# One value burst per head in sparse attention, memory-attention outputs in the transposing banks, keys and queries evicted raw

## The chip, the cores and the metric

The kernel runs on one core of one Trainium2 chip. A core has five engines that run side by side, each in its own program order: TensorE (PE; its weight loads are shown as PEld), VectorE (DVE), ScalarE (ACT), GpSimd (POOL) and SyncE (SP), which issues most of the weight DMAs. TensorE writes its results to PSUM, which has eight banks of 128 x 512 float32; ACT and DVE take them from there to SBUF. The metric is the device time of one execution in microseconds. Three runs of the kernel before took 2106.66, 2106.75 and 2107.36 us; the median is 2106.75 us.

## The reference, cut to what matters

Two decoder layers over 512 tokens of width 1024. Each layer has a mixer of three branches (sparse attention "NSA", HGRN2, gated delta net), a cross attention over 256 memory tokens, and a gated MLP with a short convolution. The change touches the sparse attention and the memory attention:

```python
# sparse attention: 8 heads in 2 groups, head width 64
q = apply_rope(rmsnorm(q, q_norm));  k_* = apply_rope(rmsnorm(k_*, k_norm))   # k_cmp, k_sel, k_win
p_cmp = masked_softmax(q @ kc.T * scale);   o_cmp = p_cmp @ vc     # 31 compressed blocks
p_sel = masked_softmax(q @ k_sel.T * scale); o_sel = p_sel @ v_sel # top 16 of 8 blocks: all, causal
p_win = masked_softmax(q @ k_win.T * scale); o_win = p_win @ v_win # window 512: causal
o = g0 * o_cmp + g1 * o_sel + g2 * o_win
# memory attention: 4 heads of width 128, 256 memory tokens
q = rmsnorm(h @ w_q, q_norm); k = rmsnorm(mem_k, k_norm)
o = softmax(q @ k.T * scale) @ mem_v;  x = x + o @ w_o
# rmsnorm(x, g) = x * rsqrt(mean(x * x) + 1e-6) * g, and h itself is rmsnorm(x)
```

## The kernel before, in words

Activations are held feature-major: 128 features by 512 tokens a tile. A dense product (`dense`, `fm_proj`) splits each weight tile into a high and a low float32r part (`load_w`: the tile `wh` by ACT, `wl` by DVE) and each activation likewise (tiles `act`), and issues three 128x512 matmuls per 128 input features into a PSUM tile `pd`. The layer's first norm is not applied to the activations before the product: its factor per token is multiplied in when the product is evicted (`fm_scaled`: one DVE multiply of `pd` by the tile `rb`). `norm.r` holds the same factors as one column per block of 128 tokens.

PSUM is cut into three pools: `pd` has 3 banks (dense products), `pa` has 2 (attention scores, attention outputs, recurrences), `pt` has 3 (transposes and small sums).

The mixer runs the delta net, then HGRN2 woven with the key side of NSA (`nsa_pre`: head norms, rotary embedding, the compressing MLP, and the split of the keys into high and low parts `KH`, `KL`), then the projections of the gates and of the NSA queries (`nsa_queries`), one branch, then the attention (`nsa_attn`). The head norm (`head_rs`) squares the projected tiles on ACT, sums them with tiny matmuls, transposes the sums and takes a reciprocal square root with small DVE instructions.

`nsa_attn` goes over four blocks i of 128 queries and, in each, over four pairs j of heads (one head of each group g). Each step of j (called a head below; there are 32 in the two layers) has two branches `br` (selected, window) and two groups, so four score tiles: two matmuls and a mask matmul into `pa`, a maximum on DVE, an exponential on ACT into a tile `pr`, a scaling on DVE. Each `pr` is then transposed in 128x128 pieces into one `pt` bank, copied by ACT to a new tile `pT`, and used in the value products. The output bank `po` comes from `pa`; its first two products are those of the compressed branch (tile `vcpad`), then come those of the values (tile `tok`). Each value product fills 64 of the array's columns (`128*64` in the profile), and group 0 and group 1 use the two halves.

The order of instructions on each engine isn't written out by hand. A scheduling layer sets it from the dependencies, the ring of buffers of each pool and priorities: code under `tc.high_priority(...)` is put ahead of other ready work. Dense matmuls of the gate projections (`gate`) that don't depend on the attention are put between its steps.

`xattn` does the same with 4 heads over 256 memory tokens: `queries`, `attend`, `finish`. In `finish`, two `pt` banks take the transposed probabilities, DVE copies the first and ACT the second to SBUF, and the product with `memV` goes to a `pa` bank, from which `split` makes the high and low parts for the output projection.

The lines that the prediction follows: L235 is every matmul (`mm`), L242 every ACT activation (`act`), L245 every two-tensor operation, L254 every scalar-tensor-tensor, L1099 the transposes of the sparse attention, L1352 and L1353 transposes and copies of the memory attention.

Of the kernel before, what the change touches and what calls it, by code (L numbers as in the profile page):

```python
# [9 lines left out]
F32 = mybir.dt.float32  # L10
# [9 lines left out]
P = 128  # L20
T = 512
NT = T // P
# [176 lines left out]
def tile_trunk(ctx, tc, a, out, dbg=None):  # L199
# [47 lines left out]
    def ts(o, x, s1, s2, op0, op1=None, eng=None):  # L247
        if op1 is None:
            (eng or V).tensor_scalar(o, x, s1, None, op0)
        else:  # L250
            (eng or V).tensor_scalar(o, x, s1, s2, op0, op1)
# [159 lines left out]
            TE.transpose(ps[:, i * rw:(i + 1) * rw], rows[:, i * P:(i + 1) * P], ident[:rw, :rw])  # L411
        return ps[:, :n * rw].rearrange("p (i c k) -> p i c k", c=nt, k=32)[:, :, :, :nh]

    def head_rs(srcs, nh, scale, eps, post=1.0, nt=NT):
        n = len(srcs) * nt * nh
        v = small(n)
        ts(v.rearrange("p (i c h) -> p i c h", c=nt, h=nh), head_sums(srcs, nh, nt), scale, eps, MUL, ADD)
        return rsqrt(v, n, post=post)

    def spread(r, i, nh, nt=NT, ps=None):  # L420
        ps = pt() if ps is None else ps
# [23 lines left out]
    def fm_scaled(norm, src, o=None):  # L445
        ps = fm_proj(norm, src)
        o = chain() if o is None else o
        with tc.high_priority(PRI2):
            tt(o, ps, norm.rb, MUL)
        return o  # L450

    gdn_S = [cst.tile([P, P], F32, name=f"gdnS{i}") for i in range(2)]
# [452 lines left out]

    NSA_K, NSA_Q = ("nkc", "nvc", "nks", "nkw"), ("nq0", "nq1", "nq2", "nq3")

    def nsa_pre(l, st):
        mark("nsa")
        rope = [chain(), chain()]  # L910
        for i in range(2):
# [4 lines left out]
        raw = box["nsa"]  # L916

        def rope_norm(idx, gains, post):
            r = head_rs([raw[i] for i in idx], 2, 1.0 / 64, EPS, post)
            for n_, i in enumerate(idx):  # L920
                t_ = raw[i]
                stt(t_, t_, gains[n_], spread(r, n_, 2), MUL, MUL)
                sh = tl("tg", NTG)
                V.stream_shuffle(sh, t_, SWAP16)
                tt(t_, t_, rope[0], MUL)
                tt(sh, sh, rope[1], MUL, eng=G)
                tt(t_, t_, sh, ADD)
# [54 lines left out]
        for br, n_ in ((0, "nks"), (1, "nkw")):  # L982
            for g_ in range(2):
                rw, ow = halves(g_)
                hi, lo = tl("chain", NCHAIN, dt=FR), tl("chain", NCHAIN, dt=FR)
                src = raw[n_][rw]
                act(hi[rw], src)
                tt(lo[rw], src, hi[rw].bitcast(F32), SUB)
                act(hi[ow], src)
                tt(lo[ow], src, hi[rw].bitcast(F32), SUB)  # L990
                KH[br, g_], KL[br, g_] = hi, lo
        yield
        compress(1, raw["nvc"])
        st.update(KH=KH, KL=KL, kcT=kcT)

    def nsa_queries(l, st):
        mark("nsa_q")
        raw, rope, halves = box["nsa"], st["rope"], st["halves"]
        r = head_rs([raw[f"nq{k}"] for k in range(4)], 2, 1.0 / 64, EPS, 0.125)
        r8 = tl("r8", 1, (P, NT, 8))  # L1000
        for c in range(NT):
            V.tensor_copy(r8[:, c].rearrange("p (g j) -> p j g", g=2),
# [23 lines left out]
    def nsa_attn(l, tok, y, st):  # L1026
# [6 lines left out]
        for i in range(NT):  # L1033
# [35 lines left out]
            for j in range(4):  # L1069
# [22 lines left out]
                for g_ in range(2):  # L1092
                    for br in range(2):
                        x_ = 2 * g_ + br
                        pr = prs[x_]
                        ts(pr[:, :W], pr[:, :W], den[:, x_:x_ + 1], None, MUL)
                        pst = pt()
                        for k in range(i + 1):
                            TE.transpose(pst[:, k * P:(k + 1) * P], pr[:, k * P:(k + 1) * P], ident)  # L1099
                        pT = chain()  # L1100
                        act(pT[:, :W], pst[:, :W])
                        hd[g_, br] = pT
                po = pa()
                o_ = [po[g_ * 64:(g_ + 1) * 64, :P] for g_ in range(2)]
                for g_ in range(2):
                    mm(o_[g_], vcpad[g_][:, j, :], pc[:, g_ * P:(g_ + 1) * P], start=True, stop=False)
                for br, off in ((0, TOK_VS), (1, TOK_VW)):
                    for k in range(i + 1):
                        for g_ in range(2):
                            mm(o_[g_], tok[:, k, off + g_ * 64:off + g_ * 64 + 64], hd[g_, br][:, k * P:(k + 1) * P],  # L1110
                               start=False, stop=(br == 1 and k == i))
                act(y[j][:, qs_], po[:, :P])
                yield

# [92 lines left out]
    def mixer(l, norm):  # L1207
# [13 lines left out]
        g2 = hgrn(l, tok)  # L1221
        next(g2)
        mark("nsa_proj")
        box["nsa"] = {n_: fm_scaled(norm, w_fm(l, n_), tl("gate", NGATE)) for n_ in NSA_K}
        st = {}
        g3 = nsa_pre(l, st)
        weave(g2, g3)
        mark("z_proj")
        for n_ in ("cz", "hg"):
# [35 lines left out]
        for n in range(QPOS):  # L1265
            gate("c", n)
        mark("nsa_qproj")
        box["nsa"].update({n_: fm_scaled(norm, w_fm(l, n_), tl("gate", NGATE)) for n_ in NSA_Q})
        mark("gates_c")
        for n in range(QPOS, KD):  # L1270
            gate("c", n)
        nsa_queries(l, st)
        mark("branch")
        branch("c", 2, hc, 2)
        ya = [chain() for _ in range(4)]
# [22 lines left out]
    def xattn(l, norm):  # L1298
# [48 lines left out]
        def finish(i, prs):  # L1347
            pT = [chain() for _ in range(2)]
            for m in range(2):
                pst = pt()  # L1350
                for c in range(NT):
                    TE.transpose(pst[:, c * P:(c + 1) * P], prs[c][:, m * P:(m + 1) * P], ident)  # L1352
                (S.copy if m else V.tensor_copy)(pT[m], pst)  # L1353
            po = pa()
            for m in range(2):
                mm(po, memV[m][:, i * P:(i + 1) * P], pT[m], start=(m == 0), stop=(m == 1))
            o.append(split(po, None, "chain", NCHAIN))

        q, prs = {}, {}
        for i in range(6):  # L1360
# [82 lines left out]
```

## Time and profile before

| what | value |
|---|---|
| median of 3 runs | 2106.75 us |
| the profiled execution's own time | 2107.62 us |
| its span, first to last instruction | 2105.8 us |
| PE busy in the span | 2055.6 us (98%) |
| DVE, ACT, POOL busy | 1436.6, 952.2, 132.7 us |
| mean granted TensorE clock | 0.995 of full speed |
| sparse attention, layer 0 and layer 1 | 366 to 553.5 and 1399 to 1586.5 us |

The profile lists each instruction with its start, its length, its engine, its line and its tiles (out<-in, buffer numbers left out). Matmuls overlap in the array, and the end of a matmul is modelled, so the busy time of PE says little on how fast it goes: what a group of matmuls costs is read from the start of its first to the start of what follows on PE. A float32 matmul that is no transpose stands in the trace as two records (so 384 instructions of the value products make 768 records).

### The profile page before, as it was taken

The numbers are of one execution on the slowest core, as the hardware profiler recorded it, in microseconds if no ns is written. First come the engines' busy times: TensorE is split into PE (matmuls) and PEld (weight loads), VectorE is DVE, ScalarE is ACT, GpSimd is POOL, SyncE is SP. The second block draws the span as 40 slices with busy tenths as digits, with TensorE's granted clock in tenths as the row PEclk, the third lists the DMA queues.
The fourth block names the chain that finished last, engine by engine and source line by source line (L and its number), as shares of the span: only waits on it lengthen the run. The fifth ranks groups of instructions, "written<-read, shape, count | busy, mean of one in ns | idle before, by whom it ended". The sixth has DMA issues, their size and how long they took to land. (4 is left out here: it accounts for less than half of the span.)

```text
span 2105.8 us, 31108 instructions
## 1 busy us (share of the span) xinstructions
PE 2055.6 (98%) x11396; PEld 1611.4 (77%) x11400; DVE 1436.6 (68%) x3052; ACT 952.2 (45%) x1868; POOL 132.7 (6%) x120
## 2 busy tenths in 40 slices
PE   8999999999999999999999998999999999999999
PEld 7877777777786788888888776777778767888887
DVE  6774898666656887377548469975666578755873
ACT  6434434555545544244444244445554454433442
POOL 2000122000010100000000003110000110000000
PEclk9999999999999999999999999999999999999999
DMA  7332222111241233323432312121113412333333
GB/s 238 90 101 71 76 72 61 56 51 46 61 136 47 94 94 95 95 95 96 119 107 78 101 41 91 56 76 51 41 46 91 128 58 90 96 93 98 95 98 108
DMA packets 118826, 180.91 MB, mean 86 GB/s; under 512 B 19920, under 2 KB 40528, under 8 KB 118672
## 3 DMA queue, kind: packets, MB, share of 16 engines
q1 hardware_dynamic: 91008, 158.64, 24.8%
q10 hardware_dynamic: 27584, 19.97, 3.2%
q8 instruction: 90, 1.47, 0.3%
q14 instruction: 64, 0.52, 0.1%
q0 software_dynamic: 80, 0.29, 0.0%
HBM read 170.21 MB, written 8.65 MB: 85 GB/s over the span
## 5 line engine op out<-in xcount | busy, mean ns | idle before, releaser
L235 PE MATMUL pd<-act,wh 128*128 128x512 f32 x3008 | 984.4, 403 | 1.4 <-DVE act L254 1.0
L242 ACT ACTIVATE wh<-wr 128x512 fp32r<-128x512 f32 (+3 forms) x600 | 368.1, 614 | 660.2 <-PE pd L235 578.3
L235 PEld LDWEIGHTS pd<-act,wh 128*128 128x128 f32 x3008 | 559.9, 189 | 133.6 <-issue 15.6
L235 PE MATMUL pd<-act,wl 128*128 128x512 f32 x1504 | 605.8, 403 | 3.0 <-DVE wl L245 3.0
L245 DVE TENSOR_TENSOR wl<-wr,wh 128x512 fp32r<-128x512 f32 (+3 forms) x600 | 409.7, 684 | 209.5 <-ACT wh L242 202.3
L235 PE MATMUL pd<-chain,wh 128*128 128x512 f32 x1344 | 426.1, 397 | 3.4 <-DVE gate L254 3.2
L235 PEld LDWEIGHTS pd<-act,wl 128*128 128x128 f32 x1504 | 284.1, 189 | 72.4 <-issue 7.1
L235 PEld LDWEIGHTS pd<-chain,wh 128*128 128x128 f32 x1344 | 251.9, 189 | 63.0 <-DVE gate L254 3.6
L235 PE MATMUL pd<-chain,wl 128*128 128x512 f32 x672 | 267.3, 398 | 0.9 <-DVE wl L245 0.9
L245 DVE TENSOR_TENSOR gate<-pd,rb 128x512 f32<-128x512 f32 x168 | 116.1, 691 | 103.9 <-PE pd L235 101.7
L235 PE MATMUL pa<-chain,chain 128*64 128x64 f32 (+7 forms) x1248 | 158.0, 294 | 4.6 <-DVE tiny L1340 3.8
L235 PEld LDWEIGHTS pd<-chain,wl 128*128 128x128 f32 x672 | 126.9, 189 | 32.2 <-DVE wl L245 2.9
L254 DVE SCALAR_TENSOR_TENSOR gate<-gate,vec,gate 128x510 f32<-128x510 f32 (+1 forms) x176 | 131.7, 750 | 18.9 <-ACT gate L242 15.9
L235 PEld LDWEIGHTS pa<-chain,chain 128*64 128x64 f32 (+3 forms) x1248 | 109.7, 162 | 43.1 <-issue 16.1
L1083 DVE TENSOR_REDUCE tiny<-pa 128x1 f32<-128x128 f32 (+3 forms) x128 | 61.2, 488 | 81.5 <-PE pa L235 81.2
L242 ACT ACTIVATE chain<-pa,tiny,r 128x128 f32<-128x128 f32 (+3 forms) x128 | 78.8, 616 | 60.9 <-DVE tiny L245 56.4
L245 POOL TENSOR_TENSOR chain<-chain,t 128x512 f32<-128x512 f32 x30 | 40.9, 1362 | 1015.7 <-ACT t L242 1015.7
L242 ACT ACTIVATE chain<-pt 128x512 f32<-128x512 f32 (+3 forms) x156 | 61.0, 444 | 65.0 <-PE pt L1099 37.1
L242 ACT ACTIVATE gate<-gate,vec 128x512 f32<-128x512 f32 x88 | 63.9, 726 | 27.0 <-DVE gate L245 27.0
L245 DVE TENSOR_TENSOR chain<-pd,chain 128x512 f32<-128x512 f32 x64 | 43.7, 688 | 37.0 <-PE pd L235 36.6
L235 PE MATMUL pa<-chain,tok 128*64 128x128 f32 x704 | 62.3, 282 | 0.0
L254 DVE SCALAR_TENSOR_TENSOR t<-t,gate 128x512 f32<-128x512 f32 x88 | 60.6, 688 | 1.9 <-ACT t L242 0.4
(238 smaller groups left out, 2006.4 us busy)
## 6 DMA issues: line engine op xcount, KB each, us to landing
wr<-in_w_fm SPq DMA_DIRECT2D x184, 256.0 KB, 2.7
wr<-in_w_up SPq DMA_DIRECT2D x176, 256.0 KB, 2.6
wr<-in_w_dn SPq DMA_DIRECT2D x64, 256.0 KB, 2.7
wr<-in_w_mix SPq DMA_DIRECT2D x32, 256.0 KB, 2.7
wr<-in_w_dn SPq DMA_DIRECT2D x32, 192.0 KB, 2.4
wr<-in_w_tk SPq DMA_DIRECT2D x16, 272.0 KB, 3.0
wr<-in_w_kv SPq DMA_DIRECT2D x16, 256.0 KB, 3.5
chain<-in_cmp_w SPq DMA_DIRECT2D x16, 256.0 KB, 4.0
```

Source lines behind the costliest of these rows:

```text
L235: TE.matmul(out_, lhsT, rhs, start=start, stop=stop, skip_group_check=True)
L242: S.activation(o, i, f, **kw)
L245: (eng or V).tensor_tensor(o, x, y, op)
L254: V.scalar_tensor_tensor(o, x, s, y, op0, op1)
L1083: V.tensor_reduce(nm, ps[:, :W], AX.X, MAX, negate=True)
```

## The change

Five edits, in both layers.

1. In `nsa_attn` the copy of the transposed probabilities goes back into the tile that was transposed (`pr`) and no new tile is taken. The value products of a head are issued with a dependency of the first of them on the last of the four copies, the two products of the compressed branch stand last, and the output bank comes from `pt`.
2. In `xattn`, `finish`: both copies and the split of the output run at high priority, and the output bank comes from `pt`.
3. Keys (`nkc`, `nks`, `nkw`) and the four query tiles are evicted by `fm_plain`: a plain ACT copy at high priority in place of the DVE multiply by `rb`. `nvc` stays as it was.
4. `head_rs` with `row=norm.r` puts the norm's factor in afterwards, on small tiles: v = sum * (row * row * scale) + eps, and the result times row.
5. The second half of each key's low part is copied from the first by ACT; before, DVE computed it again.

```diff
-    def head_rs(srcs, nh, scale, eps, post=1.0, nt=NT):
+    def head_rs(srcs, nh, scale, eps, post=1.0, nt=NT, row=None):
         n = len(srcs) * nt * nh
         v = small(n)
-        ts(v.rearrange("p (i c h) -> p i c h", c=nt, h=nh), head_sums(srcs, nh, nt), scale, eps, MUL, ADD)
-        return rsqrt(v, n, post=post)
+        v4 = lambda t_: t_.rearrange("p (i c h) -> p i c h", c=nt, h=nh)
+        if row is None:
+            ts(v4(v), head_sums(srcs, nh, nt), scale, eps, MUL, ADD)
+            return rsqrt(v, n, post=post)
+        b4 = lambda t_: t_.rearrange("p (i c h) -> p i c h", i=1, h=1).to_broadcast([P, len(srcs), nt, nh])
+        sq = small(nt)
+        stt(sq, row, scale, row, MUL, MUL)
+        tt(v4(v), head_sums(srcs, nh, nt), b4(sq), MUL)
+        ts(v, v, eps, None, ADD)
+        r = rsqrt(v, n, post=post)
+        tt(v4(r), v4(r), b4(row), MUL)
+        return r
...
+    def fm_plain(norm, src, o):
+        ps = fm_proj(norm, src)
+        with tc.high_priority(PRI2):
+            act(o, ps)
+        return o
...
-            r = head_rs([raw[i] for i in idx], 2, 1.0 / 64, EPS, post)
+            r = head_rs([raw[i] for i in idx], 2, 1.0 / 64, EPS, post, row=norm.r)
...
                 act(hi[ow], src)
-                tt(lo[ow], src, hi[rw].bitcast(F32), SUB)
+                act(lo[ow], lo[rw].bitcast(F32))
...
-        r = head_rs([raw[f"nq{k}"] for k in range(4)], 2, 1.0 / 64, EPS, 0.125)
+        r = head_rs([raw[f"nq{k}"] for k in range(4)], 2, 1.0 / 64, EPS, 0.125, row=norm.r)
...
-                        pT = chain()
-                        act(pT[:, :W], pst[:, :W])
-                        hd[g_, br] = pT
-                po = pa()
+                        copied = S.activation(pr[:, :W], pst[:, :W], AF.Copy)
+                        hd[g_, br] = pr
+                po = pt()
                 o_ = [po[g_ * 64:(g_ + 1) * 64, :P] for g_ in range(2)]
-                for g_ in range(2):
-                    mm(o_[g_], vcpad[g_][:, j, :], pc[:, g_ * P:(g_ + 1) * P], start=True, stop=False)
                 for br, off in ((0, TOK_VS), (1, TOK_VW)):
                     for k in range(i + 1):
                         for g_ in range(2):
-                            mm(o_[g_], tok[:, k, off + g_ * 64:off + g_ * 64 + 64], hd[g_, br][:, k * P:(k + 1) * P],
-                               start=False, stop=(br == 1 and k == i))
+                            m_ = TE.matmul(o_[g_], tok[:, k, off + g_ * 64:off + g_ * 64 + 64],
+                                           hd[g_, br][:, k * P:(k + 1) * P],
+                                           start=(br == 0 and k == 0), stop=False, skip_group_check=True)
+                            if br == 0 and k == 0:
+                                tc.add_manual_dep(m_.ins, copied.ins.name, mybir.DependencyInfo(
+                                    mybir.DependencyClass.Sync, mybir.DependencyReason.DATA), reason="one burst")
+                for g_ in range(2):
+                    mm(o_[g_], vcpad[g_][:, j, :], pc[:, g_ * P:(g_ + 1) * P], start=False, stop=True)
...
-        box["nsa"] = {n_: fm_scaled(norm, w_fm(l, n_), tl("gate", NGATE)) for n_ in NSA_K}
+        box["nsa"] = {n_: (fm_scaled if n_ == "nvc" else fm_plain)(norm, w_fm(l, n_), tl("gate", NGATE)) for n_ in NSA_K}
...
-        box["nsa"].update({n_: fm_scaled(norm, w_fm(l, n_), tl("gate", NGATE)) for n_ in NSA_Q})
+        box["nsa"].update({n_: fm_plain(norm, w_fm(l, n_), tl("gate", NGATE)) for n_ in NSA_Q})
...
-                (S.copy if m else V.tensor_copy)(pT[m], pst)
-            po = pa()
+                with tc.high_priority(PRI2):
+                    (S.copy if m else V.tensor_copy)(pT[m], pst)
+            po = pt()
...
-            o.append(split(po, None, "chain", NCHAIN))
+            with tc.high_priority(PRI2):
+                o.append(split(po, None, "chain", NCHAIN))
```

What the scheduler makes of it stands in the order of each engine. The next two pieces are PE before, in the first head of the first layer: `act,wh` and `act,wl` are dense gate products, `vcpad` the compressed branch, `cm,chain` transposes of probabilities, `chain,tok` value products.

```order
L235 MATMUL pd_5276<-act_247,wh_5279 128x512
L235 MATMUL pa_3934<-tg_3873,vcpad_86 64x128
L235 MATMUL pa_3934<-tg_3873,vcpad_87 64x128
L235 MATMUL pd_5276<-act_246,wl_5280 128x512
L235 MATMUL pd_5276<-act_290,wh_5279 128x512
```

```order
L235 MATMUL pd_5276<-act_335,wh_5297 128x512
L1099 MATMUL pt_3930<-cm,chain_3910 128x128
L235 MATMUL pa_3934<-chain_3917,tok_533 64x128
L235 MATMUL pa_3934<-chain_3927,tok_533 64x128
L235 MATMUL pa_3934<-chain_3922,tok_533 64x128
L235 MATMUL pa_3934<-chain_3932,tok_533 64x128
L235 MATMUL pd_5276<-act_334,wl_5298 128x512
```

The same head now, from its last transposes on:

```order
L1115 MATMUL pt_3931<-cm,chain_3909 128x128
L235 MATMUL pd_5220<-act_335,wh_5241 128x512
L1115 MATMUL pt_3935<-cm,chain_3918 128x128
L235 MATMUL pd_5220<-act_334,wl_5242 128x512
L235 MATMUL pd_5220<-act_378,wh_5241 128x512
L1123 MATMUL pt_3938<-chain_3891,tok_533 64x128
L1123 MATMUL pt_3938<-chain_3909,tok_533 64x128
L1123 MATMUL pt_3938<-chain_3900,tok_533 64x128
L1123 MATMUL pt_3938<-chain_3918,tok_533 64x128
L235 MATMUL pt_3938<-tg_3881,vcpad_86 64x128
L235 MATMUL pt_3938<-tg_3881,vcpad_87 64x128
L235 MATMUL pd_5220<-act_379,wh_5241 128x512
```

The head's 64-column products stood in two places and now stand in one, and two dense matmuls stand between the last transpose and the first value product.

DVE before, where the queries of the first layer end and the first branch begins: `gate<-pd,rb` is the eviction of a projection, `wl` the low part of a weight tile, `chain<-gate,chain` a low part of the queries, `small` the head norm, `gate<-gate,pd` the eviction that frees a dense bank.

```order
L245 TENSOR_TENSOR wl_3773<-wr_3770,wh_3772 128x512
L245 TENSOR_TENSOR gate_3449<-gate_3449,chain_2344 128x512
L245 TENSOR_TENSOR chain_3730<-gate_3371,chain_3730 64x512
L245 TENSOR_TENSOR gate_3449<-gate_3449,tg_3719 128x512
L251 TENSOR_SCALAR small_3648<-pt_3676 128x32
L245 TENSOR_TENSOR chain_3736<-gate_3410,chain_3736 64x512
L329 TENSOR_SCALAR small_3682<-small_3648 128x32
L245 TENSOR_TENSOR chain_3742<-gate_3449,chain_3742 64x512
L251 TENSOR_SCALAR small_3684<-small_3682 128x32
L254 SCALAR_TENSOR_TENSOR gate_3172<-gate_3172,pd_3754 128x512
```

DVE at the same place now:

```order
L245 TENSOR_TENSOR wl_3781<-wr_3778,wh_3780 128x512
L245 TENSOR_TENSOR gate_3453<-gate_3453,chain_2344 128x512
L245 TENSOR_TENSOR gate_3453<-gate_3453,tg_3727 128x512
L245 TENSOR_TENSOR small_3652<-pt_3682,tiny_3653 128x32
L254 SCALAR_TENSOR_TENSOR gate_3176<-gate_3176,pd_3762 128x512
L249 TENSOR_SCALAR small_3652<-small_3652 128x32
L245 TENSOR_TENSOR chain_3750<-gate_3453,chain_3750 64x512
L329 TENSOR_SCALAR small_3689<-small_3652 128x32
```

The eviction that frees the dense bank has moved up past the low parts of two queries, since earlier evictions of the queries are no longer on this engine.

## Rows read from the trace of the kernel before

**Rows 1.** Windows: length, busy of PE, PEld, DVE, ACT, POOL, clock, DMA.

```profile
230.00:330.00 100.00, 93.14 (x619) 71.11 (x618) 93.42 (x210) 41.36 (x79) 27.99 (x25) 0.98 0.24 73
366.00:553.50 187.50, 187.50 (x1183) 138.57 (x1182) 117.68 (x345) 101.77 (x265) 0.00 (x0) 1.00 0.16 49
...
1262.00:1362.00 100.00, 91.18 (x605) 68.92 (x603) 92.04 (x208) 39.98 (x77) 26.39 (x24) 0.98 0.24 72
1399.00:1586.50 187.50, 187.28 (x1180) 137.97 (x1180) 117.13 (x338) 101.31 (x265) 0.00 (x0) 1.00 0.16 49
```

**Rows 2.** Windows of the attention, instructions of tile `tok` alone (value products).

```profile
366.00:553.50 187.50, 27.23 (x320) 20.04 (x320) 0.00 (x0) 0.00 (x0) 1.00 0.16 49
```

**Rows 3.** The same for tile `vcpad` (compressed branch).

```profile
366.00:553.50 187.50, 7.03 (x64) 3.16 (x64) 0.00 (x0) 0.00 (x0) 1.00 0.16 49
```

**Rows 4.** Timeline of PE: start, length, engine, line, tiles, form, count.

```profile
391.76 0.40 PE L235 MATMUL pd<-act,wh 128*128 128x512 f32 x1
392.08 0.44 PE L235 MATMUL pa<-tg,vcpad 128*64 128x128 f32 x4
392.45 0.50 PE L235 MATMUL pd<-act,wh 128*128 128x512 f32 x1
392.79 0.39 PE L235 MATMUL pa<-chain,chain 128*128 128x256 f32 x2
```

**Rows 5.** Timeline of PE, a head whose value products are split.

```profile
472.39 0.43 PE L235 MATMUL pa<-chain,tok 128*64 128x128 f32 x2
472.75 0.50 PE L235 MATMUL pd<-act,wh 128*128 128x512 f32 x1
473.19 1.52 PE L235 MATMUL pa<-chain,tok 128*64 128x128 f32 x22
474.64 0.62 PE L235 MATMUL pa<-chain,chain 128*128 128x384 f32 x2
```

**Rows 6.** Timeline of PE, dense matmuls alone (between the rows: x2).

```profile
683.56 0.40 PE L235 MATMUL pd<-chain,wl 128*128 128x512 f32 x1
...
684.27 0.39 PE L235 MATMUL pd<-chain,wl 128*128 128x512 f32 x1
```

**Rows 7.** Timeline, a head of the last query block.

```profile
524.62 1.95 PE L1099 MATMUL pt<-cm,chain 128*128 128x128 f32 x16
525.25 2.06 ACT L242 ACTIVATE chain<-pt 128x512 f32<-128x512 f32 x4 [2.66 <-PE pt L1099]
526.50 2.35 PE L235 MATMUL pa<-chain,tok 128*64 128x128 f32 x32
```

**Rows 8.** ACT by form: count, busy us, mean ns, idle before.

```profile
L242 ACT ACTIVATE chain<-pt 128x128 f32<-128x128 f32 x32 | 7.5, 275 | 7.6 <-PE pt L1099 7.2
L242 ACT ACTIVATE chain<-pt 128x384 f32<-128x384 f32 x32 | 13.5, 494 | 11.6 <-PE pt L1099 11.6
L242 ACT ACTIVATE chain<-pa,tiny,r 128x512 f32<-128x512 f32 x32 | 24.9, 778 | 16.6 <-DVE tiny L245 14.3 <-DVE tiny L1290 2.1
L242 ACT ACTIVATION_READ_ACCUMULATOR chain<-pa,tiny,r 128x1 f32 x128 | 25.0, 196 | 0.0
L242 ACT ACTIVATE chain<-pd 128x512 f32<-128x512 f32 x8 | 4.7, 584 | 0.2
```

**Rows 9.** DVE by form, window 230 to 330.

```profile
L245 DVE TENSOR_TENSOR gate<-pd,rb 128x512 f32<-128x512 f32 x9 | 6.2, 690 | 0.3 <-PE pd L235 0.2
L245 DVE TENSOR_TENSOR chain<-gate,chain 64x512 fp32r<-64x512 f32 x8 | 5.5, 684 | 0.1
L254 DVE SCALAR_TENSOR_TENSOR tiny<-tiny,tiny 128x16 f32<-128x16 f32 x6 | 1.6, 260 | 0.1
```

**Rows 10.** Waits of PE, window 350 to 358.

```profile
PE pd L235 <- DVE gate L254: 3.2, 1, 3.2
```

**Rows 11.** Waits of PE, window 230 to 330.

```profile
PE pa L235 <- DVE chain L245: 4.8, 4, 2.7
```

**Rows 12.** Timeline of PE in the memory attention.

```profile
665.60 4.51 PE L235 MATMUL pa<-chain,chain 128*128 128x512 f32 x8 [1.89 <-DVE tiny L1340]
```

More of the change, by code (lines that the diff above doesn't have):

```diff
@@ L906, in tile_trunk, with nsa_pre @@
     NSA_K, NSA_Q = ("nkc", "nvc", "nks", "nkw"), ("nq0", "nq1", "nq2", "nq3")
-    def nsa_pre(l, st):
+    def nsa_pre(l, st, norm):
         mark("nsa")
@@ L994, in nsa_pre, with nsa_queries @@
         st.update(KH=KH, KL=KL, kcT=kcT)
-    def nsa_queries(l, st):
+    def nsa_queries(l, st, norm):
         mark("nsa_q")
         raw, rope, halves = box["nsa"], st["rope"], st["halves"]
-        r = head_rs([raw[f"nq{k}"] for k in range(4)], 2, 1.0 / 64, EPS, 0.125)
+        r = head_rs([raw[f"nq{k}"] for k in range(4)], 2, 1.0 / 64, EPS, 0.125, row=norm.r)
         r8 = tl("r8", 1, (P, NT, 8))
@@ L1223, in mixer @@
         mark("nsa_proj")
-        box["nsa"] = {n_: fm_scaled(norm, w_fm(l, n_), tl("gate", NGATE)) for n_ in NSA_K}
+        box["nsa"] = {n_: (fm_scaled if n_ == "nvc" else fm_plain)(norm, w_fm(l, n_), tl("gate", NGATE)) for n_ in NSA_K}
         st = {}
-        g3 = nsa_pre(l, st)
+        g3 = nsa_pre(l, st, norm)
         weave(g2, g3)
@@ L1271, in mixer @@
             gate("c", n)
-        nsa_queries(l, st)
+        nsa_queries(l, st, norm)
         mark("branch")
```

## The prediction

> **What bounds the kernel now.** I read the windows first, one for each stage that the change touches. In the two stretches of sparse attention PE is busy throughout (187.5 and 187.3 of 187.5 us, full granted clock) while DVE has 118 and ACT 102 us of work [rows 1]. So there PE sets the pace, and what the change takes out of PE's own sequence comes off the time. The stretch of HGRN2 and the NSA keys is different: DVE is busy 93.4 of 100 us in the first layer and 92.0 in the second, and PE stands 6.9 and 8.8 us [rows 1]; what leaves DVE there may let PE stand less.
>
> Then I read the timeline of PE inside the attention, since a busy PE can still go slowly. In a run of dense matmuls alone three take 684.27 - 683.56 = 0.71 us, 0.237 each (the row at 683.56 and the two that begin in between) [rows 6]. Around two products of the compressed branch (four records) the dense matmul in front takes 392.08 - 391.76 = 0.32, the products 0.37, the dense matmul behind 0.34 [rows 4]. The reader should see that such a visit of 64-column products costs on both sides: 0.08 in front and 0.10 behind, 0.18 in all. A dense matmul between two visits takes 473.19 - 472.75 = 0.44, which is both sides at once [rows 5]. Inside a visit the first and last products are dear and the rest cheap: two pairs of records take 0.37, eleven pairs 474.64 - 473.19 = 1.45, so a further pair costs (1.45 - 0.37) / 9 = 0.12, while one pair alone takes 472.75 - 472.39 = 0.36 [rows 4, 5]. The price of 384 products (768 records) thus depends on the number of pieces they are cut into.
>
> **Edit 1, one burst.** In the order of before I count 54 pieces of value products and 32 of the compressed branch, 86 visits in 32 heads; in the order of after there are 32, one a head. The products are the same.
>
> Inside the visits, per layer: the spans add up to 27.23 us for the values and 7.03 for the compressed branch [rows 2, 3]. A span is longer than the time to what follows by 0.44 - 0.37 = 0.07 us [rows 4], and there are 43 visits, so the products hold PE for 34.26 - 43 x 0.07 = 31.2 us. After, block i has heads of 4(i + 1) + 2 = 6, 10, 14 and 18 pairs; at 0.37 + 0.12 for each pair above two these are 0.85, 1.33, 1.81 and 2.29 us, 6.28 together, times four heads 25.1 us. Saved: 6.1 us a layer, 12.2 in both. At the edges: 54 visits fewer at 0.18 are 9.7 us. Edit 1 gives 21.9 us on PE, and in these stretches nothing else ends last.
>
> Against that stands the new wait. The first value product now waits for the last of four copies, and PE keeps its order, so everything behind it waits too: scores of the next head and dense products. In the last block before, sixteen transposes began at 524.62, ACT's first copy at 525.25 and the four copies took 2.06 us, to 527.31 [rows 7]. The transposes left PE free 1.88 us after their start (526.50). After, the order puts two to six dense or score matmuls between the last transpose and the burst. In a head of the last block with two dense and one score matmul of the same width, that is about 3 x 0.237 = 0.71 us, so PE is there at 1.88 + 0.71 = 2.59 us from the first transpose, and the copies end at 2.69. For shorter rows the copies take 275 to 494 ns [rows 8] and two or three dense matmuls (0.47 to 0.71 us) stand in between. So the wait is between nothing, where four or more matmuls stand in between, and 0.2 us, if a semaphore's way is added. I take 0.1 us for each of 32 heads, 3 us. What it costs without this cover: 527.31 - 526.50 = 0.8 us a head in the last block.
>
> The price of a wait at the head of PE's queue can be seen in the memory attention: PE stood 1.89 us before the group at 665.60 and nothing ran in between, although dense products followed behind it [rows 12]. The Trainium skill, "TensorE: Matmul & The Clock Gate", section "Step-by-step: what each phase is for", says that matmuls stay in program order and only weight loads are pulled ahead. The trace agrees with its 1.89 us. If matmuls could pass a waiting one, the 3 us would be nothing and the sum 3 us lower.
>
> Copying in place adds no instruction: four copies a head as before, into another tile. The output bank from `pt` leaves `pa`'s two banks to the scores alone; in exchange five tiles a head go through three `pt` banks. PE is fully busy here now, so I give the freer scores nothing; if the transposes of the next head had to wait for the copy of the output (a 128x128 copy, 275 ns), 32 x 0.3 = 9 us would be lost at most. The order puts scores or dense work there, and I take 0.
>
> **Edits 3 to 5, keys and queries.** DVE loses per layer seven evictions of 690 ns and four low parts of 684 ns [rows 9]: 4.8 + 2.7 = 7.6 us, of which 2.07 + 2.74 = 4.8 in the keys' stretch and 2.8 in the queries'. It gains three more small instructions in each of two head norms, at most 6 x 0.26 = 1.6 us [rows 9]. Net relief: 4.0 us in the keys' stretch, 2.0 in the queries'. ACT gains seven copies of 584 ns [rows 8] and four 64-row copies; it is 41% busy in the keys' stretch [rows 1], which hides them. Without that cover they cost 4.1 us, and by my estimate 2.4 more for the half tiles at the same price, a layer. What does PE get? In the keys' stretch it waited 4.8 us, four times, for tiles from DVE [rows 11], by the order at the HGRN2 levels, which share DVE with the keys. At the queries it stood 3.2 us because the eviction that frees a dense bank stood in DVE's queue behind low parts of the queries [rows 10]; this eviction now stands two of these earlier. The gain lies between a loss of 6.5 us a layer (ACT's copies on the path) and the whole relief, 6.0. I take 2 us a layer for the keys, half of the relief, since other HGRN2 work is late next, and 1 us once for the queries: 5 us. The head norm's longer chain (0.8 us) lies beside dense products.
>
> **Edit 2, memory attention.** The wait of 1.89 us before 665.60 was ended by DVE at L1340, a reciprocal of the softmax [rows 12]; by the order DVE's copy of the transposed probabilities stands shortly before it, and behind the head norm's small instructions. With the output in `pt` and the copies preferred one reason for the wait goes. But the order of after puts a score of the last head ahead of that output, and this score waits for a `pa` bank, which the exponentials of the head before free late. DVE's copy stands behind the same two maxima as before. A preferred copy can also hold up an exponential (0.6 us for each of 4 heads, from the 584 ns of [rows 8]). So the gain is between -2.4 and 1.9 us a layer: I take 0.5, 1 us in both.
>
> **Sum.** -21.9 + 3 - 5 - 1 = -24.9 us, against the profiled execution's 2107.62 (its span 2105.8 and 1.8 around it): 2082.7 us. The median of the runs is 0.9 lower than that execution, so I forecast 2082 us.
>
> **Rivals.**
> *Only the inside is saved.* The edges are paid at other places, since scores and transposes now stand in more pieces (130 pieces of scores in the order, 108 before), and DVE's relief reaches nothing on PE. For it: the long visit of [rows 5] ends at scores, an edge that I priced by the row of a dense matmul. Then -12.2 + 3 = -9.2: 2097 us.
> *Everything is saved.* The bursts find their copies done, the memory attention's 1.9 us go twice, and DVE's relief comes through in full in both layers: -21.9 - 3.8 - 12.0 = -37.7: 2069 us. For it: DVE is 92 to 93% busy in the keys' stretch. Against: its waits there are few and long, of one kind.
> *The burst waits for ACT, slower.* If in each head an exponential with its accumulator read (778 + 196 ns [rows 8]) runs ahead of the last copy, the burst waits 0.97 us more, 32 times: 31 us, and the sum is -21.9 + 31 = +9: 2116 us. It decides from 0.7 us a head on. For it: in some heads the order has an exponential between the third and fourth copy. Against: in those four or more matmuls stand in front of the burst, and the scheduler gives them as cover.
> *No change.* What PE saves in the attention it spends waiting for weight tiles or evictions, as the splits on ACT and DVE become the pace: 2107 us. Against: both have over 69 us free in each attention stretch.
>
> **How the numbers follow.** Forecast 0.62, between 2075 and 2090; only the inside 0.15; everything 0.12; the burst waits 0.05; no change 0.06. A range from 2069 to 2098 us leaves out the last two, about half of the second's lower side and a little of the first's upper side, about 0.2. What this measurement can tell from no change is 0.2%, 4.2 us. Faster: 0.62 + 0.15 + 0.12 = 0.89. Same: 0.06. Slower: 0.05.
>
> **What would show it right or wrong.** In the profile after, the value and compressed products (tiles `tok` and `vcpad`) should each stand in one group a head with eight to thirty-two and four records, without a dense matmul between them, and the attention should take about 9.5 us less in each layer (178 of 187.5). A wait of PE for ACT's copy of more than 0.3 us in front of the bursts would show the third rival. PE's idle time from 230 to 330 us should fall from 6.9 to near 5. The wait at the memory attention should stay above 1 us. I would be wrong if the attention's stretch kept its length with the pieces gone (then the edges were never the bursts'), or if the delta net, which isn't edited but whose order shifts a little, lost or won more than 4 us.

## The result and the profile after

| | median us | against before |
|---|---|---|
| before | 2107.03 (4 runs) | |
| after | 2082.76 (2080.20 to 2085.22, 4 runs) | ratio 0.9889 [0.9876, 0.9902], some 24 us faster |

The profiled execution of after took 2080.20 us (span 2078.4). I forecast 2082.

The two kernels shift dense matmuls between stages, so equal clock times don't hold equal work. I compare a stretch that begins with the first attention score and ends at the first residual of the mixer: the windows show the same PE instructions in it (1320 to 1322), 553 of them dense (554 in layer 1 after). Columns as in [rows 1]; before:

```profile
367.40:588.30 220.90, 220.66 (x1321) 164.93 (x1320) 143.90 (x383) 116.24 (x290) 0.00 (x0) 1.00 0.18 55
1399.90:1621.40 221.50, 221.05 (x1320) 164.87 (x1320) 143.86 (x379) 116.08 (x290) 0.00 (x0) 1.00 0.19 56
```

After; the third line holds the tile `tok` alone, the fourth `vcpad`, which answer to [rows 2, 3]. (The 384 products, 768 records, of the two layers are those of both tiles: 320 products of the values and 64 of the compressed branch.)

```profile
366.10:577.20 211.10, 209.92 (x1321) 161.20 (x1320) 142.51 (x381) 114.73 (x290) 0.00 (x0) 1.00 0.19 58
1381.00:1592.60 211.60, 209.71 (x1322) 161.30 (x1321) 142.29 (x380) 114.66 (x290) 0.00 (x0) 1.00 0.20 59
...
366.10:577.20 211.10, 21.00 (x320) 17.14 (x320) 0.00 (x0) 0.00 (x0) 1.00 0.19 58
...
366.10:577.20 211.10, 6.22 (x64) 4.05 (x64) 0.00 (x0) 0.00 (x0) 1.00 0.19 58
```

The attention is 9.8 and 9.9 us shorter: 19.7 of the 24. A first burst in the timeline of PE after:

```profile
379.05 0.40 PE L235 MATMUL pd<-act,wh 128*128 128x512 f32 x1
379.37 0.66 PE L1123 MATMUL pt<-chain,tok 128*64 128x128 f32 x8
379.86 0.39 PE L235 MATMUL pt<-tg,vcpad 128*64 128x128 f32 x4
380.18 0.50 PE L235 MATMUL pd<-act,wh 128*128 128x512 f32 x1
```

One group a head, no dense matmul inside. Its two spans overlap by 379.37 + 0.66 - 379.86 = 0.17 us and the second runs 0.07 past the next start; 16 times 0.24 taken off 21.00 + 6.22 leaves 23.4 us in which the products hold PE. Before it was 31.2. Sums over the trace, of each visit from its first start to the next start on PE, give 23.38 and 31.25.

The memory attention before (two layers), then after, in windows of equal work:

```profile
627.20:677.80 50.60, 48.55 (x238) 34.67 (x237) 33.56 (x134) 26.71 (x67) 0.00 (x0) 0.97 0.21 65
1660.30:1709.20 48.90, 46.84 (x238) 33.92 (x237) 33.53 (x134) 26.80 (x67) 0.00 (x0) 1.00 0.22 68
```

```profile
616.10:663.60 47.50, 46.20 (x238) 33.99 (x236) 33.64 (x133) 26.32 (x67) 0.00 (x0) 1.00 0.22 67
1631.70:1679.30 47.60, 46.31 (x238) 33.99 (x236) 33.65 (x133) 26.33 (x67) 0.00 (x0) 1.00 0.22 67
```

At the same granted clock (layer 1) it is 1.3 us shorter. Keys and queries together, before and then after, from the end of the delta net to the first score (362 and 364 dense matmuls):

```profile
221.10:367.40 146.30, 136.26 (x874) 104.67 (x875) 133.29 (x291) 65.14 (x120) 34.92 (x29) 0.98 0.24 73
```

```profile
220.20:366.10 145.90, 135.08 (x876) 104.27 (x875) 130.28 (x292) 69.20 (x128) 33.72 (x29) 0.99 0.24 72
```

DVE has 3.0 us less to do, the stretch is as good as unchanged. In layer 1 it takes 154.1 us before and 154.0 after, with 6.2 us less on DVE and eight dense matmuls more in it (409 for 401), some 1.9 us of work, which the run of edits 3 to 5 alone (below) doesn't show as a gain. PE's waits there before were the lines of [rows 10, 11], 4.8 and 3.2 us, and two more of 1.3 and 0.7. After (columns: engine, tile and line, releaser, total, times, longest):

```profile
PE pa L235 <- DVE chain L245: 4.6, 4, 2.7
PE pa L235 <- DVE kcT L245: 1.9, 1, 1.9
PE pt L439 <- ACT tx L242: 1.2, 1, 1.2
```

and six more of 3.0 us together: 10.0 us before, 10.7 after. The 3.2 us for a dense bank are gone; others stand in their place.

### The profile page after: what moved, and what is told of

It reads as the page before. It is cut to its first block, busy times and chain, and to the rows that moved or that the text cites. A ratio compares the mean times of both kernels' runs of the same rounds, so it can differ in the third digit from the quotient of the medians.

```text
span 2078.4 us, 31215 instructions
## 1 busy us (share of the span) xinstructions
PE 2028.8 (98%) x11400; PEld 1603.8 (77%) x11400; DVE 1420.4 (68%) x3042; ACT 959.3 (46%) x1890; POOL 131.1 (6%) x120
## 5 line engine op out<-in xcount | busy, mean ns | idle before, releaser
L245 DVE TENSOR_TENSOR gate<-pd,rb 128x512 f32<-128x512 f32 x154 | 106.4, 691 | 92.7 <-PE pd L235 90.1
L235 PE MATMUL pa<-chain,chain 128*64 128x64 f32 (+7 forms) x1216 | 143.2, 285 | 4.5 <-ACT chain L242 3.0
L254 DVE SCALAR_TENSOR_TENSOR gate<-gate,vec,gate 128x510 f32<-128x510 f32 (+1 forms) x176 | 131.7, 750 | 18.7 <-ACT gate L242 15.7
L235 PEld LDWEIGHTS pa<-chain,chain 128*64 128x64 f32 (+3 forms) x1216 | 102.9, 161 | 37.7 <-ACT chain L242 15.4
L1116 ACT ACTIVATE chain<-pt 128x128 f32<-128x128 f32 (+3 forms) x128 | 48.1, 438 | 31.1 <-PE pt L1115 24.2
L245 POOL TENSOR_TENSOR tg<-tg,chain 128x256 f32<-128x256 f32 (+1 forms) x42 | 44.8, 1074 | 201.0 <-ACT tg L242 72.2
```

The lines of the kernel that those rows point to most:

```text
L235: TE.matmul(out_, lhsT, rhs, start=start, stop=stop, skip_group_check=True)
L245: (eng or V).tensor_tensor(o, x, y, op)
L254: V.scalar_tensor_tensor(o, x, s, y, op0, op1)
L1116: copied = S.activation(pr[:, :W], pst[:, :W], AF.Copy)
```

## The experiments

Theory 1: PE is paid per piece of 64-column products, first and last pair and edges. Its rival: the edges are paid elsewhere, and part of the gain is that of the other edits. Medians of before in the three groups of runs were 2106.08 (first four), 2104.78 (next four) and 2107.26 (last three).

**Edit 1 alone** (the burst put into the kernel before).

> Edit 1 alone on the kernel before. Theory 1, visits: the gain is the 54 visits of 64-column products that go. In the trace after, the products themselves hold PE 7.8 us less a layer and their edges 7.7 us less, and at equal dense work the stretch of queries and attention is 12.5 and 11.4 us shorter; so 2107 - 24 = 2083 us, at most 3 us off. Theory 2, DVE relief: the second layer's 8 us in the delta net and the keys come from edits 3 to 5, and the attention gives only what is seen between the last HGRN2 output and the first residual (5.5 and 6.8 us): 2107 - 12 = 2095 us.

Measured 2088.53, ratio 0.9911 [0.9896, 0.9926]: about -18.7. The stretch of the attention:

```profile
368.50:578.70 210.20, 209.64 (x1321) 161.37 (x1320) 142.02 (x383) 114.85 (x290) 0.00 (x0) 1.00 0.19 58
1388.90:1600.30 211.40, 209.78 (x1321) 161.16 (x1320) 142.21 (x379) 114.73 (x290) 0.00 (x0) 1.00 0.20 59
```

10.7 and 10.1 us shorter than before; the spans of `tok` and `vcpad` are those of after. This is the edit that carries the change.

**Edits 3 to 5 alone** (keys and queries raw).

> Edits 3 to 5 alone (keys and queries evicted raw by ACT, norm factor in the head norm, low half of the keys copied by ACT). Theory 1, visits: nearly nothing, 2103 to 2107 us, since PE's waits there are few. Theory 2, DVE relief: 2095 to 2099 us. My forecast had 5 us for this part: 2102.

Measured 2106.45, ratio 1.0000 [0.9991, 1.0008]: nothing. The wait for a dense bank is gone here too, and this stands among the waits of keys and queries:

```profile
PE pa L235 <- DVE kcT L245: 3.0, 1, 3.0
```

**Edit 2 alone** (memory attention).

> Edit 2 alone (memory attention: output in the pt banks, copies and split preferred). In the trace after, this stage is 2.9 us shorter in the first layer and 0.6 in the second. Theory 1: 2103 to 2106 us. Theory 2: the same. If the bank was what held it: 3.8 us, 2103; if the score ahead takes over the wait: 2106 to 2107.

Measured 2101.90, ratio 0.9980 [0.9971, 0.9989]: -4.2. PE's wait there is the same as after:

```profile
PE pa L235 <- ACT chain L242: 1.3, 1, 1.3
```

One caution on its profile: the delta net of layer 1, with nothing edited, is 3.2 us shorter than before, at another granted clock. Before, then this run:

```profile
1097.20:1229.50 132.30, 128.06 (x948) 101.67 (x948) 83.36 (x200) 51.71 (x102) 5.13 (x6) 0.97 0.28 80
```

```profile
1095.40:1224.50 129.10, 125.42 (x947) 99.88 (x948) 83.36 (x200) 51.71 (x102) 5.13 (x6) 1.00 0.29 81
```

PE is busy 2.6 us less there, at the higher clock, and its wait for a DMA is 0.5 shorter (3.0 for 3.5). So 3.2 us of the profiles' difference are not the edit's. The ratio, from ten runs of this kernel, is what counts.

**Of edit 2 the bank alone**: the output comes from `pt`; the copies and the split have no priority (what they "keep" in the expectation is the order of before).

```diff
-            po = pa()
+            po = pt()
```

> Of edit 2 alone the bank: the output of the memory attention comes from pt, the copies and the split keep their priority. Edit 2 as a whole took 1.3 us out of each layer's memory attention at full clock (48.9 to 47.5 us in layer 1) and the wait in front of it went from 1.9 us on DVE's reciprocal to 1.3 us on ACT's exponential. Theory 1, the bank does it (the output no longer takes a pa bank from the scores): -2 to -3 us against before, 2102 to 2104 us. Theory 2, the priorities do it: no change, 2105 to 2107 us.

Measured 2102.45, ratio 0.9979 [0.9971, 0.9988]: all of edit 2's gain. PE's wait is the same 1.3 us for ACT's exponential.

**Two visits a head**: the compressed products first, in a visit of their own, then the burst of values.

> The kernel after with the two products of the compressed branch issued first again and free of the burst, so that they make a visit of their own in most heads: 58 to 64 visits for 32, all else as after. Theory 1, visits: each costs its two edges (0.2 to 0.24 us) and the dear first and last pair (0.13 us), so 28 to 32 times 0.33 to 0.37 us: 9 to 12 us slower than after, 2092 to 2095 us. Rival: it is the bank and the copies in place that gained, not the number of visits: as after, 2083.

Measured 2089.06, ratio 0.9916 [0.9902, 0.9930]: 0.27% or some 6 us above the change, between the rival's nothing and theory 1's 9 to 12. `vcpad` alone is back at 7.03 us a layer, and the stretch is 5.1 and 4.5 us longer than after, which is theory 1's size; why the time is not longer by all of it stays open. Layer 0:

```profile
366.00:582.20 216.20, 215.05 (x1321) 161.62 (x1320) 142.77 (x380) 114.72 (x290) 0.00 (x0) 1.00 0.19 57
```

**Without the added dependency.**

```diff
-                            if br == 0 and k == 0:
-                                tc.add_manual_dep(m_.ins, copied.ins.name, ...)
```

> The change in full without the added dependency of the first value product on the last copy. In the order the value products then stand in 54 pieces again (32 with the dependency, 54 before), but the compressed products stay behind the last of them and open no visit of their own (86 visits before). Theory 1, what is paid is the number of pieces: 22 pieces more at 0.13 us inside (0.37 for two pairs against 0.24 as part of a longer piece) and 0.10 at the entry are +5 us over the change: about 2087 us. Theory 2, the dependency brings nothing and the gain is that of the order of the two kinds and of the banks: 2080 to 2084 us. If the wait for the copies cost 3 us, as the prediction has it, it would take about as much off the 5.

Measured 2098.86, ratio 0.9970 [0.9960, 0.9981]: 17 us over the change, three times what theory 1 gave. From start to start the visits hold PE 28.1 us a layer (23.4 in the change) and the transposes 20.3 (16.9), since 14 visits a layer begin right behind a transpose here and none in the change. Together these are 16.3 of the 16.4 us by which the two stretches are longer.

Theory 1 had the price of a piece wrong. By the order the first value product of 11 heads a layer stands alone. Alone it takes 0.36 us, like the one of [rows 5], and the burst behind it, which lacks this product on one half of the columns, is no shorter. A burst of the last block, 17 products:

```profile
522.37 1.85 PE L1123 MATMUL pt<-chain,tok 128*64 128x128 f32 x29
...
524.48 0.23 PE L235 MATMUL pa<-negb,identb 128*128 128x128 bf16 x1
```

It takes 2.11 us, as 18 products do in the change (below). The single products are 4.0 of the 4.7 us a layer. In some other heads the burst waits for a copy in its middle. The head of the burst above, here (PE, and ACT's last two copies):

```profile
381.12 0.64 ACT L1116 ACTIVATE chain<-pt 128x128 f32<-128x128 f32 x2
381.38 0.76 PE L1123 MATMUL pt<-chain,tok 128*64 128x128 f32 x7
...
381.87 0.28 PE L235 MATMUL pt<-tg,vcpad 128*64 128x128 f32 x1
...
381.98 0.27 PE L1123 MATMUL pt<-chain,tok 128*64 128x128 f32 x1
...
382.40 0.50 PE L235 MATMUL pd<-act,wl 128*128 128x512 f32 x1
```

The same six products in the same order take 1.02 us from first to next, 0.81 with the dependency. They begin before the last copy has ended (381.76), the last value product waits in the middle, and a compressed product (381.87) starts ahead of a value product's last record (381.98) although it stands behind it in the order. This suggested the next experiment.

**Groups one after the other**: a burst first does all value products of group 0, then those of group 1.

```diff
-                for br, off in ((0, TOK_VS), (1, TOK_VW)):
-                    for k in range(i + 1):
-                        for g_ in range(2):
+                for g_ in range(2):
+                    for br, off in ((0, TOK_VS), (1, TOK_VW)):
+                        for k in range(i + 1):
```

> The change, but within a burst all value products of group 0 come first and then those of group 1; in the change the two groups alternate, and they use different halves of the array's columns. In the change two records begin 6 to 8 ns apart and the next two 0.10 us later. Theory 1, the two that begin together belong to different groups, so the halves work side by side only where the groups alternate: 192 products a layer at 0.11 us go up to 0.2, +17 us a layer, about 2117 us. Theory 2, the two belong to one product (its two float32 passes): no change, 2080 to 2085 us.

Measured 2104.62, ratio 0.9988 [0.9979, 0.9997]: 21 us over the change, with not one instruction more. Theory 1 in kind, two thirds of its size. From start to start the visits hold PE 34.5 us a layer, 23.4 in the change. A burst of the last block:

```profile
525.95 3.00 PE L1123 MATMUL pt<-chain,tok 128*64 128x128 f32 x29
528.69 0.32 PE L235 MATMUL pt<-tg,vcpad 128*64 128x128 f32 x1
528.79 0.27 PE L1123 MATMUL pt<-chain,tok 128*64 128x128 f32 x1
...
529.43 0.74 PE L235 MATMUL pa<-chain,chain 128*128 128x512 f32 x2
```

3.48 us, where the change takes 2.11 (below). At 528.69 a compressed product starts while value products that stand ahead of it in the order are still to start (528.79); they can only be on the other half: each half of the columns goes on by itself. In the first block, where each group has two value products, nothing is lost:

```profile
382.15 0.66 PE L1123 MATMUL pt<-chain,tok 128*64 128x128 f32 x8
...
382.97 0.50 PE L235 MATMUL pd<-act,wh 128*128 128x512 f32 x1
```

These are 0.82 us, 0.81 in the change. Bursts of 10, 14 and 18 products take 1.73, 2.60 and 3.48 us on average, 1.24, 1.68 and 2.12 in the change. So two products of one group in a row still leave both halves at work, with four and more a half falls idle; that the first block is spared is one reason why theory 1 was too high. The Trainium skill, "TensorEngine Tiling (Array Packing)", section "Key Properties", says that different tiles can load and multiply in parallel; the 21 us agree.

**Each copy done twice.**

```diff
                         copied = S.activation(pr[:, :W], pst[:, :W], AF.Copy)
+                        act(pr[:, :W], pst[:, :W])
```

> The change in full, but ACT copies each of the 128 transposed tiles twice, one copy behind the other into the same tile: the last copy of a head ends 0.28 to 0.58 us later. Theory 1, the wait in front of the bursts has cover to spare: 0 to +3 us over the change, 2082 to 2086 us. Theory 2, the cover is as thin as the prediction has it (0.1 us): the mean copy of 0.43 us is waited for in each of 32 heads, +14 us: 2096 us.

Measured 2078.19, ratio 0.9876 [0.9862, 0.9889]: no slower, and below what either theory gave. ACT has 19.5 us more to do and the stretch is 0.5 us shorter than after:

```profile
369.50:580.10 210.60, 209.57 (x1321) 160.47 (x1320) 142.36 (x380) 134.25 (x354) 0.00 (x0) 1.00 0.19 59
```

A head of the last block there: behind the last transposes (521.94) stand eight dense matmuls, not three as in the change, and the burst still comes right behind the last copy (523.19 + 1.15 = 524.34).

```profile
521.94 0.66 PE L1115 MATMUL pt<-cm,chain 128*128 128x128 f32 x4
...
523.19 1.15 ACT L1117 ACTIVATE chain<-pt 128x512 f32<-128x512 f32 x2
...
524.39 1.97 PE L1124 MATMUL pt<-chain,tok 128*64 128x128 f32 x32
```

**Only the queries raw**, the keys as before.

> The change with the keys as before (scaled by DVE at the eviction, low part computed twice): only the queries keep the raw eviction. In the traces so far the stretch of the keys, less 0.232 us for each dense matmul in it, is 2.1 us longer with the change in layer 0 and 0.6 us shorter in layer 1, while the stretch of the queries is 2.7 and 1.4 us shorter. Theory 1, the keys' part costs or brings nothing and the queries' part alone brings about 3 us: 2078 to 2083 us. Theory 2, what the queries' part saves is only moved: as edits 1 and 2 together, 2106.1 - 18 - 4 = 2084 us or more.

Measured 2082.49, ratio 0.9894 [0.9880, 0.9907]: the change itself, within the interval. Neither part of edits 3 to 5 can be told from nothing.

**One burst for two heads.**

> One burst for each two heads: both heads' scores, transposes and copies first, then both heads' products, 16 visits in all instead of 32. Theory 1, pieces: 16 fewer at 0.13 us inside and 0.10 at the entry are -3.7 us, and the way back to dense matmuls at 0.08 to 0.10 up to 1.6 more: 2077 to 2079 us. Rival: what is gathered moves dense matmuls out of the attention to its end, where weights are waited for, and the ring of transposing banks is held longer, so it is not faster than the change: 2082 to 2090 us.

Measured 2075.70 (2075.25 to 2076.11), ratio 0.9862 [0.9848, 0.9875]: faster than the change, theory 1, by some 6 us. The stretch is 2.0 and 2.5 us shorter than after, without a wait for copies; the visits hold PE 22.5 us a layer from start to start (23.4 in the change):

```profile
366.90:576.00 209.10, 207.73 (x1322) 161.05 (x1321) 143.43 (x381) 115.22 (x290) 0.00 (x0) 1.00 0.19 59
```

**One burst for four heads.**

> One burst for each four heads, 8 visits in all (16 with two heads, 32 in the change). Theory 1, pieces: against the burst of two heads 8 visits fewer at 0.23 us, -1.8, and 84 fewer returns to dense matmuls in the order at 0.084 us, up to -7: 2067 to 2074 us. Rival: with a whole block gathered the scores and transposes lose the dense matmuls that hide ACT and DVE, PE waits for exponentials and copies, and the time is 2076 us or more.

Measured 2152.15, ratio 1.0215 [1.0196, 1.0234]: 45 us slower than before: the rival, 76 us above its bound. The stretch, and PE's longest wait in it:

```profile
368.40:615.70 247.30, 225.26 (x1321) 176.56 (x1320) 145.96 (x380) 117.91 (x290) 0.00 (x0) 0.92 0.16 50
```

```profile
PE pa L235 <- ACT chain L242: 15.6, 14, 1.8
```

PE runs out of dense matmuls to put between scores: none starts from 504.6 to 587.6 us. It waits for exponentials there, 1.0 us each time up to 515.76, 518.14 and 522.02, and then the clock falls to the lower of its two levels (1.2 for 2.4 GHz), not for the last time. From 524.4 to 530 the granted clock is 0.50, and two score matmuls take 525.44 - 524.42 = 1.02 us; from 536.7 to 540.6 it is 1.00, and they take 537.35 - 536.79 = 0.56. Of the 36 us by which the stretch is longer than after, PE stands 21 longer and is busy 15 longer.

## Why the prediction was right, and where it was not

*Inside the visits* (-12.2): 31.25 to 23.38 us a layer, -15.7 in both. The kind was right, the size short by a misreading of [rows 5]. By the order the eleven products (pairs of records) there are six on one half of the columns and five on the other. Such a visit takes as long as one of twelve, 1.45 us for 1.46 (the latter in the run with two visits a head). So a further product costs (1.45 - 0.37) / 10 = 0.11, not 0.12, and six and 18 products 0.80 and 2.10; 0.81 and 2.11 were measured (first and last block). The sign that I passed over is that one product alone takes 0.36 and two, one on each half, 0.37. My estimate from these rows: a visit in alternating order takes about 0.15 us and 0.22 more for each product on its longer half. Of the 7.9 us a layer, 2.4 are the compressed products' own visits, 3.6 ten value products that stood alone in front of their burst, and 1.8 bursts that began before their last copy had ended, as in [rows 7] (the longest 2.28 us, 1.90 in the run with two visits a head).

*The edges* (-9.7): too much, and not where I had them. I summed all records of the stretch, each from its own start to the next start on PE. Visits take 15.7 us less in the two layers, transposes 5.7 less, scores and small products 1.8 more. The dense matmuls, on which I had put the edges, take 140.9 us before and 140.8 after in layer 0, 141.5 and 141.6 in layer 1: nothing. My row [rows 4] put 0.08 and 0.10 on the visit, but a dense matmul that follows scores or transposes pays nearly the same: further below, two of them behind a mask product take 514.45 - 513.90 = 0.55, where [rows 6] give 0.47. Where a visit stood between scores and dense work, taking it away left an edge. What came off stood in front of visits that began right behind a transpose: 15 a layer before, none after. The last transpose of the first head and what follows it, before, then after:

```profile
379.16 0.33 PE L1099 MATMUL pt<-cm,chain 128*128 128x128 f32 x1
379.42 0.87 PE L235 MATMUL pa<-chain,tok 128*64 128x128 f32 x8
```

```profile
378.65 0.33 PE L1115 MATMUL pt<-cm,chain 128*128 128x128 f32 x1
378.73 0.47 PE L235 MATMUL pd<-act,wl 128*128 128x512 f32 x1
```

Value products start 0.26 us behind the start of this transpose, a dense matmul 0.08; on average of the stretch these are 0.21 and 0.04. A wait for the copies is hardly the reason: in the run with two visits a head the compressed products, which read none of them, start 0.26 us behind the same transpose, and nearly all these times are one of two values, 0.20 or 0.26, before and in that run alike. No run isolates this price. So the rival of the edges paid elsewhere was right for the dense matmuls, and wrong for the transposes.

*The new wait* (+3): about nothing. The head that answers to [rows 7], after:

```profile
512.09 1.94 PE L1115 MATMUL pt<-cm,chain 128*128 128x128 f32 x16
512.73 2.07 ACT L1116 ACTIVATE chain<-pt 128x512 f32<-128x512 f32 x4 [0.81 <-PE pt L1115]
513.87 0.22 PE L235 MATMUL pa<-negb,identb 128*128 128x128 bf16 x1
513.90 0.71 PE L235 MATMUL pd<-act,wh 128*128 128x512 f32 x2
514.45 0.39 PE L235 MATMUL pd<-act,wl 128*128 128x512 f32 x1
514.85 1.97 PE L1123 MATMUL pt<-chain,tok 128*64 128x128 f32 x32
...
516.96 0.73 PE L235 MATMUL pa<-chain,chain 128*128 128x512 f32 x2
```

The burst starts 0.05 us behind the last copy (514.80), 0.40 behind the last dense matmul, whose edge alone takes 0.32: 0.08 us of wait, as reckoned for this block. In the first block (above) the dense matmul in front takes 379.37 - 379.05 = 0.32, the bare edge. The doubled copies show why: the scheduler fits the cover to the copies. What I had not asked is what the wait buys: without the dependency 17 of the 24 us are lost, some 9 to visits, most of it to first products that stand alone, and 7 to transposes with a visit right behind them.

*Edit 1 in sum* (-18.9): -18.7 measured, inside too low, edges too high and at the wrong neighbours, wait too high. The sum was better than its terms, and that is luck.

*Keys and queries* (-5): the step that failed, 0 within 0.1%. I took half of DVE's relief for PE. By the windows the relief itself was 3.0 and 6.2 us in the two layers, where I had 6.0 in each. The waits that end last there are the keys' own chain and HGRN2's; with the one on the dense bank gone, PE came sooner to products of the compressed keys that were not ready (`kcT`, 3.0 us with edits 3 to 5 alone, 1.9 after), and it stood 10.0 us before and 10.7 after. I had the lines of [rows 11] before me, four waits for one kind of tile, and should have asked what precedes that tile rather than how busy DVE is.

*Memory attention* (-1): -4.2 [-6.1, -2.3], mis-sized. The wait stayed above 1 us, on the exponential that I had named as late next, 1.3 for 1.9. The windows show 1.3 us a layer at equal clock, 2.6 in both; the rest up to 4.2 lies within the interval. The bank does it, not the preference of the copies.

*The delta net* of layer 1, after:

```profile
1083.10:1211.20 128.10, 125.10 (x943) 99.73 (x942) 80.96 (x196) 51.28 (x103) 5.12 (x6) 0.99 0.29 81
```

This is 4.2 us shorter than the profile of before, just over the 4 that I named as a sign of being wrong. But that profile stood at 0.97 there, and the run of edit 2 alone, with the net as before and at 1.00, is 3.2 shorter already. So about 1 us is left, with five PE records fewer in the stretch.

Parts and whole agree: -18.7 - 4.2 + 0 = -22.9 against some -23.4 by the ratio. That the memory attention gave 3 more and the keys 5 less than I took is why the forecast came within 1 us: it was right in its main cause, the pieces, and lucky in how the errors of the terms cancel.

What I cited from the Trainium skill ("TensorE: Matmul & The Clock Gate", "Step-by-step: what each phase is for"), that matmuls stay in program order, needs a limit: the run with the groups one after the other shows products on one half of the columns passing those on the other. For the wait in [rows 12] it holds.

## What to carry to other kernels

Where PE is the pace, count the pieces into which narrow products are cut, and price a piece by its longer column half: a product that stands alone costs as much as two. An edge is saved only if what takes the visit's place pays less, so sum from start to start over the neighbours too. Long runs on one half leave the other idle, and one wait in front of a whole burst can be worth more than starting its first product early. Gathering pays until the engine has no other work left to cover the others: two heads gained 6 us more, four heads lost 69.

## What was not expected of the hardware

- The two 64-column halves of the array run apart: alternating products 2.11 us for a burst, the same products group by group 3.48.
- A product that stands alone on one half takes 0.36 us, two side by side 0.37; a burst that lacks one product on one half is no shorter (2.11 us for 17 as for 18).
- A visit of 64-column products starts 0.21 us behind the start of a transpose in front of it, a dense matmul 0.04 (averages of the attention stretch, before and after).
- One execution's granted clock can hide or make 2.6 us in a stage that nobody touched (0.97 against 1.00 in the delta net).
